# Where the output projection hands over to the up projection: six weight loads in a set order, and two additions of squares moved from GpSimd to VectorE

## The chip, the cores and the metric

The kernel runs on one core of one Trainium2 chip. The metric is the device time of one launch in microseconds (us). The kernel before took 2681.77 us, the median of three runs (2680.84, 2681.77 and 2685.62). Everything is computed in float32 accuracy: each float32 factor is split into a high and a low part of the matmul type fp32r, and three matmuls (high x high, high x low, low x high) make one product.

## The reference, cut to what matters

One layer of a hybrid decoder, for 512 prompt tokens and 8 x 8 sample tokens, 576 columns in all. The mixer's result `mix` goes through the output projection, the sum with the input is normalised, and the feed-forward part begins with the up projection:

```python
def _rmsnorm(x, g):
    y = xf * lax.rsqrt(jnp.mean(xf * xf, axis=-1, keepdims=True) + EPS)
    return (y * g).astype(x.dtype)
...
x = x + jnp.einsum('ble,ed->bld', mix, w_out)        # 2048 -> 2048
h = _rmsnorm(x, norm_ffn_g)
u = jnp.einsum('bld,df->blf', h, w_up)               # 2048 -> 2 x 5632
uc, ffn_new = _causal_dwconv(u, ffn_buf, ffn_conv_w)
gate, up = jnp.split(uc + ffn_conv_b, 2, axis=-1)
x = x + jnp.einsum('blf,fd->bld', jax.nn.silu(gate) * up, w_down)
```

The change touches only the passage from the first of these products to the second: the sums of squares of the new `x` (for the norm) and the first loads of `w_up`.

## The kernel before, in words

Activations lie transposed: 128 features on the partitions, 576 tokens along the free axis, 16 such tiles for 2048 features. The stages follow each other: input projection with the two recurrent heads beside it (to about 1060 us), output projection `w_out` (to about 1150 us), up projection (to about 2140 us), down projection.

**Output projection (`Layer.w_out`).** For each of 16 output tiles a PSUM tile `pd` collects the product (matmuls on line 199). `evac` then loads the input tile from `in_xT` into a buffer `r`, adds the product (VectorE, L1064), writes the sum to DRAM (`x2d`, issued by SyncE a little later through `later`, L188), squares it on ScalarE (`square_acc2`, L1133), adds the square on GpSimd to one of two running sums `acc` (L1134, even and odd tiles), and forms y = x * gain * rstd on VectorE (L1068). Two y tiles together make one group of right operands (`right_operands`): seven combinations of their halves (L1188), each split into `bh` by a ScalarE cast (L119) and `bl` by a VectorE subtraction (L120). There are eight groups. The last two output tiles are computed as a pair (`dense_pair`), so that both their PSUM tiles become complete at the end, and group 7, made of them, is the last.

**Up projection (`ffn`, `pair`, `left_operands`).** A 2 x 2 block of weights times a 2 x 2 block of activations is done in seven products instead of eight. `left_operands` forms seven weight combinations from four loads of 512 KB (a11, a21, a22, a12; L1206), with additions on VectorE (L1230) and the split into `wh` (ScalarE, L119) and `wl` (VectorE, L120). A product is 8 groups x 3 matmuls of 128 x 288 (L1265). For the first pair the first three products (weights a11, a21+a22, and that less a11) are begun on groups 0 to 6, then all three get group 7, then `norm2` puts two matmuls with a matrix of ones on TensorE (L1118), which sum the squares over the partitions; its results scale the outputs later. Then come the other four products.

**What sets the order.** TensorE's order is the order in which the program is written. The other engines' orders come from a scheduler that simulates the program with priorities (`ahead`, `urgent`); `tc.issue_after(ins)` forces what is written inside it behind `ins` on the same engine. Each engine runs its own list strictly in order.

**Buffers.** Loads of `w_up` go to two kinds of buffers: two of the pool `wp`, also used by the loads of `w_out`, and four of `ur`, which lie where the output projection's left activations `ah` and `al` lay, so they can be filled only when the last matmuls no longer read these. Before, every third load goes to `wp`. The tiles `r` of this passage come from a pool of five buffers (`rb`): two hold `acc`, three rotate.

Of the kernel before, what the change touches and what calls it, by code (L numbers as in the profile page):

```python
# [1 line left out]

# [1 line left out]

# [7 lines left out]
ALU = mybir.AluOpType  # L12
# [3 lines left out]
KT = 16  # L16
# [50 lines left out]
class Layer:  # L67
# [967 lines left out]
    def w_out(self, mix):  # L1035


        nc, I = self.nc, self.I
        V = nc.vector
# [14 lines left out]
        both = right(b1, reversed(range(KB1)))[::-1]  # L1054
        self.bh, self.bl = [], []
        self.acc = [self.r(), self.r()]
        ys = []

        def evac(pd):
            n = len(ys)  # L1060
            m = OUT_ORDER[n]
            x = self.r()
            nc.sync.dma_start(out=x, in_=I["xT"][m])
            V.tensor_tensor(out=self.v2(x), in0=self.halves(pd), in1=self.v2(x), op=ALU.add)  # L1064
            self.later(4, self.x2d[m], x)
            self.square_acc2(x, n)
            y = xo.tile([P, NT], F32, tag="y", name=self.nm("y"), bufs=4)
            V.scalar_tensor_tensor(out=y, in0=x, scalar=self.par[:, G2 + m:G2 + m + 1], in1=self.rstd, op0=ALU.mult, op1=ALU.mult)  # L1068
            ys.append(y)

        def operands(k):
            self.right_operands(*both[k], ys[2 * k], ys[2 * k + 1], self.r())

        for k in range(7):
            for i in range(2):
                evac(self.dense())
            if k < KB1:
                operands(k)
            if k == 1:
                pads = lambda t: t[:, 514:594].rearrange("p (b w) -> p b w", b=NB)  # L1080
                nc.gpsimd.memset(self.ratio[:, 0:2], 1.0)
                nc.gpsimd.memset(pads(self.ratio)[:, :, 0:2], 1.0)
                V.reciprocal(self.ratio[:, 2:514], self.rstd[:, 0:SEQ])
                V.reciprocal(pads(self.ratio)[:, :, 2:10], self.rstd[:, SEQ:NT].rearrange("p (b w) -> p b w", b=NB))
# [12 lines left out]
        with self.ahead(OPA):  # L1097
            operands(5)
            operands(6)
            with self.tc.issue_after(self.last_split[0].ins), self.tc.issue_after(self.last_split[1].ins):  # L1100
                evac(pds[0])
                next(steps)
                next(steps)
                evac(pds[1])
                next(steps)
                operands(7)
                V.tensor_tensor(out=self.acc[0], in0=self.acc[0], in1=self.acc[1], op=ALU.add)
        self.finish_jobs()
        self.close("xo")
        return steps  # L1110
# [15 lines left out]
    def square_acc2(self, x, k):  # L1126
        nc = self.nc
        acc = self.acc
        if k < 2:
            nc.scalar.activation(acc[k], x, AF.Square)  # L1130
        else:
            sq = self.r()
            nc.scalar.activation(sq, x, AF.Square)  # L1133
            nc.gpsimd.tensor_tensor(out=acc[k % 2], in0=acc[k % 2], in1=sq, op=ALU.add)  # L1134


    def conv_pads(self, f):
# [62 lines left out]
    def operands(self, early, raws):  # L1200

        def raw(j, t, u):
            pool, n = (self.ur, 4) if self.nraw % 3 else (self.wp, 2)
            self.nraw += 1
            r = raws.pop(0) if raws and n == 4 else pool.tile([P, 1024], F32, tag="raw", name=self.nm("raw"), bufs=n)
            self.nc.sync.dma_start(out=r, in_=self.I["w_up"][2 * j + t][u])  # L1206
            return r

        return self.left_operands(self.ur, 1024, [lambda t, u, j=j: raw(j, t, u) for j in range(NF)], 1, early)
# [434 lines left out]
```

## Time and profile before

| what | value |
|---|---|
| median of the runs | 2681.77 us |
| the profiled execution's own time | 2683.74 us |
| its span from first to last instruction | 2682.0 us |
| TensorE matmul busy | 2638.5 us, 98% |
| VectorE busy | 2079.1 us, 78% |
| ScalarE busy | 1094.6 us, 41% |
| GpSimd busy | 464.5 us, 17% |
| mean granted TensorE clock | 0.997 |

PE is the matmul engine, PEld its weight loads, DVE is VectorE, ACT ScalarE, POOL GpSimd, SPq the DMA queue that SyncE issues. In a timeline row stand the start and the length in microseconds, the engine, the line of the kernel, the operation and its tiles (out<-in, without buffer numbers), and in brackets how long the engine had been idle and what ended that. The lengths of instructions in a row overlap a little (the next one starts before the last has quite ended), so a cost in a chain is best read from one start to the next. TensorE is busy nearly everywhere; what idle time it has around the passage of this change lies between 1150 us and 1171 us.

### The profile page before, as it was taken

To read this page: it belongs to the slowest core of one execution; us is meant where nothing else is said; L and a number is where in the kernel's file an instruction comes from. 1 tells how busy PE (TensorE), PEld (TensorE's weight loads), DVE (VectorE), ACT (ScalarE), POOL (GpSimd) and SP (SyncE) were. 2 spreads that over 40 slices of the span, in tenths; PEclk is the share of its full clock that TensorE was granted. 3 is DMA by queue.
4 is the path that set the end of the run, shared out by engine and by line. 5 is a ranking of instruction groups with operands and counts; after the bars stand their busy time and mean duration, and the time that the engine had idled before them with its cause. 6 is when DMAs were issued, how large, how long until landed. Compare 5 with 4: busy or idle time off the path is not lost.

```text
span 2682.0 us, 48801 instructions
## 1 busy us (share of the span) xinstructions
PE 2638.5 (98%) x19895; PEld 2594.6 (97%) x19895; DVE 2079.1 (78%) x3444; ACT 1094.6 (41%) x1700; POOL 464.5 (17%) x658
## 2 busy tenths in 40 slices
PE   7999999999999999999999999999999999999998
PEld 7998999999999999989999999999999999999997
DVE  7887777765544355489999999999999998988656
ACT  5335344443333232244444444444444443434323
POOL 3222322222211001111111111111111200000001
PEclk9999999999999999999999999999999999999999
DMA  5222222222333433333333333333333373342332
GB/s 196 86 74 94 88 92 92 92 88 90 114 107 99 135 114 131 124 128 113 108 108 108 108 109 108 109 109 111 110 109 109 116 247 95 115 138 72 122 101 97
DMA packets 109865, 299.30 MB, mean 112 GB/s; under 512 B 21624, under 2 KB 27896, under 8 KB 109640
## 3 DMA queue, kind: packets, MB, share of 16 engines
q1 hardware_dynamic: 105592, 286.45, 33.2%
q0 software_dynamic: 1808, 7.37, 0.8%
q8 instruction: 156, 2.56, 0.4%
q10 hardware_dynamic: 2240, 2.36, 0.3%
q14 instruction: 69, 0.57, 0.1%
HBM read 260.07 MB, written 36.06 MB: 110 GB/s over the span
## 4 chain that ended last, share of the span: by engine, by line
PE 88%; DVE 5%; DMA 1%; issue 1%; ACT 0%; POOL 0%; DVEq 0%; SPq 0%; ACTq 0%; POOLq 0%
PE pr L1265 33%; PE pd L199 33%; PE pd L1265 13%; PE pr L199 3%; PE pr L1493 1%; DVE wl L120 1%; DVE bl L120 1%; DMA r<-hid 0%; DVE r L1528 0%; PE pr L843 0%; PE pr L257 0%; PE pr L980 0%; PE pr L982 0%; DVE r L1188 0%; PE pr L855 0%
## 5 line engine op out<-in xcount | busy, mean ns | idle before, releaser
L119 ACT CAST wh<-raw 128x1024 fp32r<-128x1024 f32 (+1 forms) x394 | 405.4, 1029 | 679.3 <-PE pd L199 361.5
L1265 PE MATMUL pr<-bh,wl 128*128 128x288 f32 x2248 | 663.0, 295 | 4.6 <-DVE wl L120 4.6
L1265 PE MATMUL pr<-bh,wh 128*128 128x288 f32 x2248 | 665.2, 296 | 1.2 <-ACT bh L119 1.2
L1265 PE MATMUL pr<-bl,wh 128*128 128x288 f32 x2248 | 662.4, 295 | 0.6 <-DVE bl L120 0.6
L120 DVE TENSOR_TENSOR wl<-raw,wh 128x1024 fp32r<-128x1024 f32 (+1 forms) x394 | 476.5, 1210 | 127.8 <-ACT wh L119 123.7
L199 PE MATMUL pd<-ah,wh 128*128 128x288 f32 x2304 | 518.6, 307 | 0.0
L199 PE MATMUL pd<-ah,wl 128*128 128x288 f32 x2304 | 493.0, 296 | 0.2 <-DVE wl L120 0.2
L199 PE MATMUL pd<-al,wh 128*128 128x288 f32 x2304 | 492.5, 295 | 0.0
L1265 PEld LDWEIGHTS pr<-bh,wl 128*128 128x128 f32 x2248 | 423.5, 188 | 5.8 <-DVE wl L120 5.8
L1265 PEld LDWEIGHTS pr<-bl,wh 128*128 128x128 f32 x2248 | 424.5, 189 | 1.1 <-DVE bl L120 1.1
L1265 PEld LDWEIGHTS pr<-bh,wh 128*128 128x128 f32 x2248 | 422.9, 188 | 1.5 <-ACT bh L119 1.5
L199 PEld LDWEIGHTS pd<-ah,wh 128*128 128x128 f32 x2304 | 369.9, 189 | 14.1 <-issue 7.7
L199 PEld LDWEIGHTS pd<-ah,wl 128*128 128x128 f32 x2304 | 370.5, 189 | 0.5 <-DVE wl L120 0.5
L199 PEld LDWEIGHTS pd<-al,wh 128*128 128x128 f32 x2304 | 370.4, 189 | 0.0
L119 ACT CAST wh<-s 128x1024 fp32r<-128x1024 f32 (+1 forms) x180 | 179.1, 995 | 373.8 <-DVE s L1230 142.5
L1265 PE MATMUL pd<-bh,wh 128*128 128x288 f32 x888 | 262.5, 296 | 0.1
L1265 PE MATMUL pd<-bh,wl 128*128 128x288 f32 x888 | 261.0, 294 | 0.8 <-DVE wl L120 0.8
L1265 PE MATMUL pd<-bl,wh 128*128 128x288 f32 x888 | 260.2, 293 | 0.0
L1148 POOL COPY fst<-r 128x18 f32<-128x18 f32 x88 | 97.6, 1109 | 679.5 <-DVE r L1304 679.5
L120 DVE TENSOR_TENSOR wl<-s,wh 128x1024 fp32r<-128x1024 f32 (+1 forms) x180 | 206.6, 1148 | 6.2 <-ACT wh L119 0.2
L1265 PEld LDWEIGHTS pd<-bh,wl 128*128 128x128 f32 x888 | 166.9, 188 | 1.0 <-DVE wl L120 1.0
L1265 PEld LDWEIGHTS pd<-bl,wh 128*128 128x128 f32 x888 | 167.3, 188 | 0.0
(398 smaller groups left out, 3787.2 us busy)
## 6 DMA issues: line engine op xcount, KB each, us to landing
raw<-in_w_up SPq DMA_DIRECT2D x176, 512.0 KB
raw<-in_w_in SPq DMA_DIRECT2D x114, 512.0 KB
raw<-in_w_down SPq DMA_DIRECT2D x40, 512.0 KB
raw<-in_w_out SPq DMA_DIRECT2D x32, 512.0 KB
raw<-in_w_down SPq DMA_DIRECT2D x40, 384.0 KB
hid<-r SPq DMA_DIRECT2D x44, 288.0 KB
r<-hid SPq DMA_DIRECT2D x40, 288.0 KB
r<-in_xT SPq DMA_DIRECT2D x32, 288.0 KB
```

The source lines that it names most:

```text
L119: self.last_split = (nc.scalar.copy(hi, src), nc.vector.tensor_tensor(out=lo, in0=src, in1=hi.bitcast(F32), op=ALU.subtract))
L120: nc.vector.tensor_tensor(out=lo, in0=src, in1=hi.bitcast(F32), op=ALU.subtract))
L199: mm(outs[hf], w, x[:, hf * HALF:(hf + 1) * HALF], start=first and i == 0, stop=last and i == 2)
L1148: nc.gpsimd.tensor_copy(f, rb[:, 512:602].rearrange("p (b w) -> p b w", b=9)[:, :, 0:2])
L1265: mm(out, w[:, ks], x[:, sl], start=k == 0 and i == 0, stop=k == nk - 1 and i == 2)
L1493: mm(pr[:, 0:n], w[:, ks], acts[kk][:, a * NT + sl.start:a * NT + sl.stop], start=kk == 0 and i == 0, stop=kk == FB - 1 and i == 2)
```

## The change

It does two things.

First, the loads. The rule for the pool of the n-th load of `w_up` changes from every third in `wp` to the first and the last of every six in `wp`; four of six go to `ur` as before. And loads 2 to 7, counted from 1, are each forced behind the one before on SyncE's queue, so that the first loads are issued in the order a11, a21, a22, a12, then a11 and a21 of the next pair, and the next.

Second, the squares. For the last two output tiles `square_acc2` still squares on ScalarE but leaves out the GpSimd addition and returns the square. Where before VectorE added `acc[1]` to `acc[0]`, now it adds the two squares and `acc[1]` to `acc[0]` one after the other, and all three additions are forced behind the last split of group 7.

```diff
@@ Layer.w_out
-        ys = []
+        ys, sq = [], []
@@ evac
-            self.square_acc2(x, n)
+            sq.append(self.square_acc2(x, n))
@@ end of w_out
                 operands(7)
-                V.tensor_tensor(out=self.acc[0], in0=self.acc[0], in1=self.acc[1], op=ALU.add)
+                with self.tc.issue_after(self.last_split[1].ins):
+                    for t in (*sq[-2:], self.acc[1]):
+                        V.tensor_tensor(out=self.acc[0], in0=self.acc[0], in1=t, op=ALU.add)
@@ square_acc2
             sq = self.r()
             nc.scalar.activation(sq, x, AF.Square)
-            nc.gpsimd.tensor_tensor(out=acc[k % 2], in0=acc[k % 2], in1=sq, op=ALU.add)
+            if k < KT - 2:
+                nc.gpsimd.tensor_tensor(out=acc[k % 2], in0=acc[k % 2], in1=sq, op=ALU.add)
+            return sq
@@ raw, in operands
-            pool, n = (self.ur, 4) if self.nraw % 3 else (self.wp, 2)
+            pool, n = (self.ur, 4) if 0 < self.nraw % 6 < 5 else (self.wp, 2)
             self.nraw += 1
             r = raws.pop(0) if raws and n == 4 else pool.tile([P, 1024], F32, tag="raw", name=self.nm("raw"), bufs=n)
-            self.nc.sync.dma_start(out=r, in_=self.I["w_up"][2 * j + t][u])
+            with self.tc.issue_after(self.last_raw.ins) if 1 < self.nraw < 8 else nullcontext():
+                self.last_raw = self.nc.sync.dma_start(out=r, in_=self.I["w_up"][2 * j + t][u])
             return r
```

In the built programs the orders move as follows. (Line numbers of the changed kernel are up to five higher: L1206 becomes L1211, L1188 L1192, L1107 L1109, L1118 L1120, L1265 L1270, L1230 L1235, L1300 L1305.)

SyncE's queue at the handover, before (12598 is a11, 12602 a12, 12557 and 12558 are a21 and a22, 12555 and 12556 the next pair's a11 and a21):

```order
L1206 DMA raw_1570_12598<-in_w_up 128x1024
L1206 DMA raw_1571_12602<-in_w_up 128x1024
L1206 DMA raw_1561_12557<-in_w_up 128x1024
L1206 DMA raw_1562_12558<-in_w_up 128x1024
L1206 DMA raw_1559_12555<-in_w_up 128x1024
L1206 DMA raw_1560_12556<-in_w_up 128x1024
```

And now (12597 is a11, 12557 a21, 12558 a22, 12555 a12, 12556 the next a11, 12727 the next a21):

```order
L1211 DMA raw_1570_12597<-in_w_up 128x1024
L1211 DMA raw_1561_12557<-in_w_up 128x1024
L1211 DMA raw_1562_12558<-in_w_up 128x1024
L1211 DMA raw_1559_12555<-in_w_up 128x1024
L1211 DMA raw_1560_12556<-in_w_up 128x1024
L1211 DMA raw_1584_12727<-in_w_up 128x1024
```

The second load into a buffer of `wp` stood second and now stands last, behind the four into `ur`.

VectorE from the last y product (L1068) on, before (r_1579 is the scratch tile of group 7, r_1399 and r_1400 are the two `acc`, s_1558 the combined weights, wl_1586 the low half of the fourth product's weights):

```order
L1068 SCALAR_TENSOR_TENSOR y_1576_12617<-r_1574_12611,par_82,rstd_90 128x576
L1188 TENSOR_TENSOR r_1579_12624<-y_1569_12596 128x288
L1107 TENSOR_TENSOR r_1399_10616<-r_1399_10616,r_1400_10617 128x576
L1188 TENSOR_TENSOR y_1569_12596<-y_1576_12617,y_1569_12596 128x288
L1188 TENSOR_TENSOR r_1579_12624<-y_1576_12617,r_1579_12624 128x288
L120 TENSOR_TENSOR bl_1564_12563<-y_1576_12617,bh_1563_12562 128x576
L120 TENSOR_TENSOR bl_1564_12563<-y_1569_12596,bh_1563_12562 128x576
L120 TENSOR_TENSOR bl_1564_12563<-r_1579_12624,bh_1563_12562 128x576
L1188 TENSOR_TENSOR y_1576_12617<-y_1576_12617,r_1579_12624 128x288
L1230 TENSOR_TENSOR s_1558_12554<-raw_1571_12602,s_1558_12554 128x1024
L120 TENSOR_TENSOR bl_1564_12563<-y_1576_12617,bh_1563_12562 128x288
L120 TENSOR_TENSOR wl_1586_12730<-raw_1571_12602,wh_1585_12729 128x1024
```

And now, from the same product to the scratch tile's first use, and from there to the third addition to `acc`:

```order
L1068 SCALAR_TENSOR_TENSOR y_1575_12614<-r_1573_12609,par_82,rstd_90 128x576
L1235 TENSOR_TENSOR s_1558_12554<-raw_1559_12555,s_1558_12554 128x1024
L120 TENSOR_TENSOR bl_1564_12563<-y_1575_12614,bh_1563_12562 128x576
L1192 TENSOR_TENSOR r_1578_12621<-y_1569_12595 128x288
L1192 TENSOR_TENSOR y_1569_12595<-y_1575_12614,y_1569_12595 128x288
```

```order
L1192 TENSOR_TENSOR r_1578_12621<-y_1575_12614,r_1578_12621 128x288
L1192 TENSOR_TENSOR y_1575_12614<-y_1575_12614,r_1578_12621 128x288
L120 TENSOR_TENSOR bl_1564_12563<-y_1569_12595,bh_1563_12562 128x576
L120 TENSOR_TENSOR bl_1564_12563<-r_1578_12621,bh_1563_12562 128x576
L120 TENSOR_TENSOR bl_1564_12563<-y_1575_12614,bh_1563_12562 128x288
L1109 TENSOR_TENSOR r_1399_10616<-r_1399_10616,r_1568_12593 128x576
L120 TENSOR_TENSOR wl_1586_12730<-raw_1559_12555,wh_1585_12729 128x1024
L1109 TENSOR_TENSOR r_1399_10616<-r_1399_10616,r_1574_12612 128x576
L120 TENSOR_TENSOR wl_1588_12735<-raw_1561_12557,wh_1587_12734 128x1024
L1109 TENSOR_TENSOR r_1399_10616<-r_1399_10616,r_1400_10617 128x576
```

A weight combination (L1235) and one split of group 7 now stand ahead of the scratch tile's first use, one addition to `acc` has become three, and two weight splits stand between these three.

TensorE's list has the same instructions in the same order; what stands in it as waits differs. Before, where group 7 ends and the two matmuls with ones (L1118) follow:

```order
L1265 MATMUL pr_1584_12654<-bh_1563_12562,wl_1578_12621 128x288
L1118 MATMUL pd_1591_12743<-r_1399_10616,ones_84 128x288 [waits PE_49]
L1118 MATMUL pd_1591_12743<-r_1399_10616,ones_84 128x288
L1265 MATMUL pr_1598_12764<-bh_1397_10614,wh_1585_12729 128x288 [waits Activation_49]
L1265 MATMUL pr_1598_12764<-bl_1398_10615,wh_1585_12729 128x288
L1265 MATMUL pr_1598_12764<-bh_1397_10614,wl_1586_12730 128x288 [waits DVE_49]
```

And now:

```order
L1270 MATMUL pr_1583_12653<-bh_1563_12562,wl_1577_12618 128x288
L1120 MATMUL pd_1591_12743<-r_1399_10616,ones_84 128x288 [waits DVE_49,PE_49]
L1120 MATMUL pd_1591_12743<-r_1399_10616,ones_84 128x288
L1270 MATMUL pr_1598_12764<-bh_1397_10614,wh_1585_12729 128x288 [waits Activation_49]
L1270 MATMUL pr_1598_12764<-bl_1398_10615,wh_1585_12729 128x288
L1270 MATMUL pr_1598_12764<-bh_1397_10614,wl_1586_12730 128x288
```

The wait on VectorE has moved from the fourth product's third matmul to the matmul with ones, three rows earlier. GpSimd's list loses two rows (the two additions), and nothing else of it changes but the order of a DMA and a memset. Behind the third pair of the up projection the orders of VectorE and ScalarE are the same as before; SyncE's differ once more at the very end of that stage, where the first load for the down projection now stands behind four loads of hidden tiles instead of ahead of them.

More of the change, by code (lines that the diff above doesn't have):

```diff
@@ L1 @@
-from contextlib import ExitStack, contextmanager
+from contextlib import ExitStack, contextmanager, nullcontext
 import numpy as np
```

## The prediction

> **What bounds the kernel now.** I read the page's busy times first, then the shares of the chain of waits, and then a table of stages around the handover.
>
> ```profile
> PE 2638.5 (98%) x19895; PEld 2594.6 (97%) x19895; DVE 2079.1 (78%) x3444; ACT 1094.6 (41%) x1700; POOL 464.5 (17%) x658
> PE 88%; DVE 5%; DMA 1%; issue 1%; ACT 0%; POOL 0%; DVEq 0%; SPq 0%; ACTq 0%; POOLq 0%
> ```
>
> TensorE sets the time. An edit elsewhere counts only where TensorE waits for it. In the next table the columns are the stretch, its length, busy time of PE, PEld, DVE, ACT and POOL (with instructions), the granted clock, the DMA share and GB/s.
>
> ```profile
> 1151.00:1155.30 4.30, 1.13 (x9) 0.90 (x8) 3.28 (x4) 1.21 (x2) 0.00 (x0) 1.00 0.64 251
> 1155.30:1158.70 3.40, 3.40 (x16) 3.40 (x15) 3.40 (x3) 0.52 (x1) 1.50 (x1) 0.50 0.53 174
> 1158.70:1164.70 6.00, 5.62 (x42) 5.39 (x41) 6.00 (x7) 2.31 (x3) 1.67 (x2) 1.00 0.49 138
> 1164.70:1171.00 6.30, 3.60 (x19) 2.48 (x18) 6.30 (x11) 4.69 (x8) 0.75 (x2) 1.00 0.00 1
> 1171.00:1180.00 9.00, 9.00 (x69) 9.00 (x70) 9.00 (x15) 4.63 (x6) 0.49 (x2) 1.00 0.65 225
> 1180.00:2060.00 880.00, 880.00 (x6641) 880.00 (x6641) 828.04 (x1111) 399.48 (x438) 171.45 (x238) 1.00 0.34 108
> ```
>
> Up to 1171 TensorE has holes while VectorE is full; from 1171 on TensorE is full for 880 us and more. So there is nothing later in which a gain is lost or a loss made good: what moves TensorE at 1171 moves the end by as much. The holes, with their releasers in brackets:
>
> ```profile
> 1154.44 0.40 PE L1265 MATMUL pr<-bh,wl 128*128 128x288 f32 x1 [3.17 <-DVE wl L120]
> 1162.20 0.40 PE L1265 MATMUL pr<-bh,wl 128*128 128x288 f32 x1 [0.38 <-DVE wl L120]
> 1166.21 0.40 PE L1265 MATMUL pr<-bh,wh 128*128 128x288 f32 x1 [1.24 <-ACT bh L119]
> 1167.21 0.40 PE L1265 MATMUL pr<-bl,wh 128*128 128x288 f32 x1 [0.60 <-DVE bl L120]
> 1168.64 1.13 PE L1118 MATMUL pd<-r,ones 128*128 128x288 f32 x4
> ...
> 1169.75 0.29 PE L1265 MATMUL pr<-bl,wh 128*128 128x288 f32 x1
> 1170.89 0.40 PE L1265 MATMUL pr<-bh,wl 128*128 128x288 f32 x1 [0.85 <-DVE wl L120]
> ```
>
> They sum to 6.24 us, all on VectorE's list or a cast behind it. The matmuls with ones, at 1168.64, carry no bracket: they wait for nothing.
>
> **Part one, the load order: 0 us.** The first hole ends on the split of a11, which VectorE runs behind the sum a21 + a22, and that sum waits for a load:
>
> ```profile
> 1140.30 0.33 SPq L1206 DMA_DIRECT2D raw<-in_w_up  x1
> 1147.03 1.76 SPq L1206 DMA_DIRECT2D raw<-in_w_up  x4
> ...
> 1155.08 0.33 SPq L188 DMA_DIRECT2D x2d<-r  x1
> 1155.50 0.38 SPq L1063 DMA_DIRECT2D r<-in_xT  x1
> 1160.41 0.33 SPq L1206 DMA_DIRECT2D raw<-in_w_up  x1
> 1161.04 0.33 SPq L188 DMA_DIRECT2D x2d<-r  x1
> ```
> ```profile
> 1152.02 1.23 DVE L1230 TENSOR_TENSOR s<-raw,raw 128x1024 f32<-128x1024 f32 x1 [5.54 <-DMA raw<-in_w_up]
> 1153.17 1.22 DVE L120 TENSOR_TENSOR wl<-raw,wh 128x1024 fp32r<-128x1024 f32 x1
> 1154.30 0.75 DVE L1064 TENSOR_TENSOR r<-pd,r 128x576 f32<-128x576 f32 x1
> ```
>
> The order now puts a21 and a22 second and third, but before they were third and fourth behind a load issued 6.7 us earlier, and both versions must wait until 1147.03 for the `ur` buffers. So they land as before and the 3.17 us stay. a12 now comes with them instead of early, needed first at about 1162. Four issues take 1.76 us, 0.44 each, so the sixth load goes out at about 1148.8 and is out of SyncE's way 6 us before the store at 1155.08. Bounds: -0.4 us (one issue pitch less ahead of a22) to +0.4; I take 0, as the wait for the buffers is the same. In the long stage the `wp` and `ur` pattern changes too; no TensorE wait stands in its 880 us, which covers it. Without that cover it is the second rival.
>
> **Part two, the squares: removed.** Two GpSimd additions lie on top of two products on VectorE:
>
> ```profile
> 1155.96 1.50 POOL L1134 TENSOR_TENSOR r<-r,r 128x576 f32<-128x576 f32 x1 [27.19 <-ACT r L1133]
> 1161.86 1.57 POOL L1134 TENSOR_TENSOR r<-r,r 128x576 f32<-128x576 f32 x1 [4.40 <-ACT r L1133]
> 1165.32 0.10 POOL L1142 MEMSET r<- 128x2 f32 x1 [1.74 <-DMA x2d<-r]
> ```
> ```profile
> 1130.12 0.81 DVE L1068 SCALAR_TENSOR_TENSOR y<-r,par,rstd 128x576 f32<-128x576 f32 x1
> ...
> 1156.10 1.98 DVE L1068 SCALAR_TENSOR_TENSOR y<-r,par,rstd 128x576 f32<-128x576 f32 x1
> 1158.00 1.21 DVE L1230 TENSOR_TENSOR s<-s,raw 128x1024 f32<-128x1024 f32 x1
> 1159.13 1.21 DVE L1230 TENSOR_TENSOR raw<-raw,raw 128x1024 f32<-128x1024 f32 x1
> ...
> 1162.07 1.97 DVE L1068 SCALAR_TENSOR_TENSOR y<-r,par,rstd 128x576 f32<-128x576 f32 x1
> 1163.97 0.44 DVE L1188 TENSOR_TENSOR r<-y 128x288 f32<-128x288 f32 x1
> 1164.34 0.74 DVE L1107 TENSOR_TENSOR r<-r,r 128x576 f32<-128x576 f32 x1
> 1165.01 0.44 DVE L1188 TENSOR_TENSOR y<-y,y 128x288 f32<-128x288 f32 x1
> ...
> 1169.62 2.34 DVE L120 TENSOR_TENSOR wl<-raw,wh 128x1024 fp32r<-128x1024 f32 x2
> 1171.90 1.21 DVE L120 TENSOR_TENSOR wl<-s,wh 128x1024 fp32r<-128x1024 f32 x1
> ```
>
> The product takes 0.81 us with GpSimd idle and 1.97 with it adding. I take 0.81: two products, 2 x 1.1 = 2.2 us off VectorE's chain, 1.1 by the first and 1.1 by the second.
>
> **Part two: added.** From start to start (the rows overlap a little) a 1024 wide operation takes 1159.13 - 1158.00 = 1.13 us, a 576 wide one 0.67, a 288 wide one 0.37. By them and the new list: first product 1156.10 to 1156.9, two combinations to 1159.17, addition of the product to the input 1159.84, split 1160.97, second product 1161.77, s + a12 1162.90, `bl` 1163.57. There the scratch tile begins, 0.4 us before the old 1163.97: the 1.1 us of the second product has gone to the sum with a12, which now stands ahead.
>
> A new wait follows. Both squares now live until the last additions, so of the five `r` buffers the scratch tile gets the one of x15, and must wait until this is stored. Before, the store was issued at 1161.04 and a GpSimd memset that waited for it ran at 1165.32, about 4.2 us later. The store is now issued when x15 is ready 0.4 earlier and the load ahead of it likewise some 1.1 earlier, at about 1159.95, and lands at about 1164.2. So the scratch tile starts between 1163.57 (no wait) and 1164.2; I take the wait.
>
> From its start to the end of the third addition: 0.37 and 0.37 until the ScalarE cast (0.67) of y14 lets `bl` go at +1.6; two `bl` 1.34, the half one 0.37, +3.31; then add, split, add, split, add: 3 x 0.67 + 2 x 1.13 = 4.27, and 0.07 until the last has quite ended: +7.65. That is 1171.2 to 1171.85. The matmuls with ones now wait for it, where before they ran at 1168.64. The fourth product's second matmul (1169.75) began 1.11 us after them; its third, whose weights are now split in time, another 0.13 (69 matmuls in 9.00 us): +1.25, so 1172.45 to 1173.1 where it was 1170.89. **That is +1.6 to +2.2; I take +1.9.** The small holes at 1162 to 1168 shift and shrink, but they lie ahead of the new hole and are swallowed by it. Behind the additions on VectorE is the next weight split, at 1171.90 before: the list now reaches it at 1171.8, no later, since the sum with a12 (1.13) has gone ahead and the addition of 0.67 before the first `bl` is gone; so nobody behind waits more. Bounds: if the product stays at 1.97 the chain is 2.2 later, +3.8; if additions and splits hide, nothing is lost (first rival).
>
> **The clock.** The hole of 3.17 us was followed by 3.40 us at a granted clock of 0.50, with 16 matmuls where 3.40 x 69/9.00 = 26 would have run: 10 x 0.13 = 1.3 us lost. The new hole stands in front of the ones. Group 7's last matmul ran until the ones at 1168.64; it now comes about 0.5 us sooner (the scratch tile starts up to 0.2 us later, but the addition of 0.67 behind it is gone), so the hole reaches from about 1168 to 1171.8, 3.8 us. The table's 1158.70:1164.70, with small holes only, kept 1.00. So the loss is 0 (it stays full) to 1.7 (half of 3.40); I take 1.3. [...]
>
> **Sum.** 2683.74 (the profiled execution's own time) + 0 + 1.9 + 1.3 = 2686.9. That execution was 1.97 above the median of the runs, so the forecast for a median is 2681.77 + 3.2 = 2685.0. One part in a thousand: 0.2% of the time, 5.4 us, is about what a measurement of this kernel can tell from no change, so this is "the same", on the slow side.
>
> **Rivals.** *The saving reaches TensorE (faster).* If the matmuls with ones do not hold the fourth product, the four later holes close: 0.38 + 1.24 + 0.60 + 0.85 = 3.07, 2678.7. For it: VectorE is the releaser of nearly all of them. Against: the ones stand ahead of that product in TensorE's list and the last addition behind two splits of 1.13. 0.08.
>
> *The long stage begins to wait (slower).* Two `wp` loads now follow each other across every second pair. Place: the loads of each pair; it decides once a load comes later than VectorE's slack, 880 - 828.04 = 52 us over 40 pairs (44 pairs from about 1172 to 2140 are 22 us each, 880/22 = 40), 1.3 us each.
>
> ```profile
> raw<-in_w_up SPq DMA_DIRECT2D x176, 512.0 KB
> ```
>
> Four loads a pair make 44 pairs; half an issue pitch (0.22 us) in each is 9.7, so 2685.0 + 9.7 = 2694.7. For it: VectorE is 94% busy. Against: the DMA share is 0.34 and nothing waits in 880 us. 0.08.
>
> *The change doesn't do what it says.* The product stays at 1.97 for another cause than GpSimd: third matmul +3.8, with the clock +5.1, 2686.9. Against: 0.81 at 1130.12. 0.06.
>
> **How the numbers follow.** Forecast 0.78, with its own range +0 to +4.5: 2681.8 to 2686.3. The first rival ends below, the third just above, the second far above. 2679.5 to 2688.5 takes in the first part of the first rival's cases, the third, and the runs' own scatter, and leaves out most of the second. Faster by over 0.2% needs less than 2676.4, more than the first rival gives: 0.03. Slower needs more than 2687.1: the second rival's 0.08 and 0.04 of upper ends. Same: 0.85.
>
> **What would show it.** Both L1068 near 0.8 us; VectorE held by the store of x15 for up to 0.6 us at the scratch tile; the matmuls with ones held by L1109 for about 4 us; a granted clock of 0.50 behind that; the 3.17 us unchanged; a full TensorE from then on. I am wrong if the ones start before 1170.5, if the first hole moves by over 0.5 us, or if a wait appears after 1180.

## The result, and the profile after

The changed kernel takes 2687.56 us, the median of 20 runs (2685.59 to 2690.93); the kernel before, in 20 runs beside it, 2683.43 (2680.84 to 2686.0). The ratio is 1.0017, 95% interval 1.001 to 1.0024: 4.1 us slower by the medians, where 3.2 were forecast. The profiled execution has a span of 2685.6 us, 3.6 more than before.

The same table of stages as in the prediction, of the changed kernel (stretch, length, busy time of PE, PEld, DVE, ACT, POOL, granted clock, DMA share, GB/s):

```profile
1151.00:1155.30 4.30, 1.26 (x9) 1.26 (x9) 3.67 (x4) 1.61 (x2) 0.00 (x0) 0.95 0.88 351
1155.30:1158.70 3.40, 3.40 (x17) 3.40 (x16) 3.40 (x4) 1.08 (x2) 0.00 (x0) 0.56 0.55 177
1158.70:1164.70 6.00, 5.23 (x40) 5.00 (x38) 5.30 (x9) 1.45 (x3) 0.00 (x0) 1.00 0.49 139
1164.70:1171.00 6.30, 2.00 (x9) 1.31 (x9) 6.27 (x11) 5.81 (x8) 0.87 (x3) 0.81 0.27 90
1171.00:1180.00 9.00, 8.28 (x46) 7.74 (x47) 8.29 (x12) 2.35 (x4) 0.33 (x2) 0.76 0.40 144
1180.00:2060.00 880.00, 880.00 (x6642) 880.00 (x6642) 825.30 (x1110) 398.70 (x437) 174.38 (x235) 1.00 0.34 108
```

From 1180 on nothing differs: TensorE is full in both, with 6642 matmuls against 6641. The loss lies before. The holes of TensorE, from its timeline:

```profile
1154.04 0.40 PE L1270 MATMUL pr<-bh,wl 128*128 128x288 f32 x1 [3.04 <-DVE wl L120]
1165.49 0.40 PE L1270 MATMUL pr<-bh,wh 128*128 128x288 f32 x1 [1.56 <-ACT bh L119]
1166.32 0.40 PE L1270 MATMUL pr<-bl,wh 128*128 128x288 f32 x1 [0.42 <-DVE bl L120]
1171.72 2.26 PE L1120 MATMUL pd<-r,ones 128*128 128x288 f32 x4 [3.80 <-DVE r L1109]
```

The first hole is as it was (3.17 before). The holes of 0.38 and 0.85 are gone, and in front of the matmuls with ones (L1120), which waited for nothing before, stands a new one of 3.80 us, ended by the third addition. In all 8.82 us against 6.24. On VectorE:

```profile
1155.70 0.81 DVE L1068 SCALAR_TENSOR_TENSOR y<-r,par,rstd 128x576 f32<-128x576 f32 x1
...
1160.50 0.81 DVE L1068 SCALAR_TENSOR_TENSOR y<-r,par,rstd 128x576 f32<-128x576 f32 x1
1161.23 1.22 DVE L1235 TENSOR_TENSOR s<-raw,s 128x1024 f32<-128x1024 f32 x1
...
1163.79 0.46 DVE L1192 TENSOR_TENSOR r<-y 128x288 f32<-128x288 f32 x1 [0.67 <-DMA x2d<-r]
...
1167.22 0.75 DVE L1109 TENSOR_TENSOR r<-r,r 128x576 f32<-128x576 f32 x1
1167.89 1.22 DVE L120 TENSOR_TENSOR wl<-raw,wh 128x1024 fp32r<-128x1024 f32 x1
1169.03 0.75 DVE L1109 TENSOR_TENSOR r<-r,r 128x576 f32<-128x576 f32 x1
1169.69 1.22 DVE L120 TENSOR_TENSOR wl<-raw,wh 128x1024 fp32r<-128x1024 f32 x1
1170.83 0.75 DVE L1109 TENSOR_TENSOR r<-r,r 128x576 f32<-128x576 f32 x1
```

Both L1068 are down from 1.97 to 0.81 us; the scratch tile waits 0.67 us for the store of x15 (`x2d<-r`); two splits lie between the three additions. And the clock, in a table of finer stages:

```profile
1167.90:1171.70 3.80, 0.02 (x1) 0.01 (x1) 3.80 (x6) 3.37 (x4) 0.74 (x2) 0.59 0.62 210
1171.70:1175.30 3.60, 3.58 (x11) 3.03 (x12) 3.60 (x5) 0.50 (x1) 0.33 (x2) 0.50 0.84 293
```

Behind the new hole TensorE runs 3.6 us at half clock. The mean of 0.59 in the hole says that the clock had fallen before the hole was over.

**A measure for the experiments.** Effects of one or two microseconds drown in the time of a launch, which scatters by five. So beside the times stands the *passage*: from the last pair of matmuls of the output projection (L199) to the ScalarE copy of the first product of the 41st pair of the up projection. All work in between is the same, TensorE sets the pace, and the first 1150 us are left out. Before and after:

```profile
1150.57 0.43 PE L199 MATMUL pd<-ah,wl 128*128 128x288 f32 x2
...
2056.08 0.39 ACT L1310 COPY p<-pr 128x288 f32<-128x288 f32 x1
```
```profile
1150.31 0.43 PE L199 MATMUL pd<-ah,wl 128*128 128x288 f32 x2
...
2059.80 0.39 ACT L1315 COPY p<-pr 128x288 f32<-128x288 f32 x1
```

905.51 and 909.49: +3.98 us. Taking the holes away leaves 899.27 and 900.67. So of 3.98 us **2.58 are holes and 1.40 are slower work**, put down here to the clock (0.50 over the 3.6 us behind the new hole). It is one execution of each kernel, and as the runs below show, the clock's part is not the same in every execution.

### The profile page after: what moved, and what is told of

It is laid out like the page before. It is cut to its first block, busy times and chain, and to the rows that moved or that the text cites. A ratio compares the mean times of both kernels' runs of the same rounds, so it can differ in the third digit from the quotient of the medians.

```text
span 2685.6 us, 48777 instructions
## 1 busy us (share of the span) xinstructions
PE 2638.9 (98%) x19895; PEld 2595.1 (97%) x19895; DVE 2078.2 (77%) x3446; ACT 1094.4 (41%) x1700; POOL 463.7 (17%) x656
## 4 chain that ended last, share of the span: by engine, by line
PE 88%; DVE 5%; DMA 1%; issue 1%; ACT 0%; POOL 0%; DVEq 0%; SPq 0%; ACTq 0%; POOLq 0%
PE pr L1270 33%; PE pd L199 33%; PE pd L1270 13%; PE pr L199 3%; PE pr L1498 1%; DVE wl L120 1%; DVE bl L120 0%; DMA r<-hid 0%; DVE r L1533 0%; PE pr L843 0%; PE pr L257 0%; PE pr L980 0%; PE pr L982 0%; DVE r L1192 0%; PE pr L855 0%
## 5 line engine op out<-in xcount | busy, mean ns | idle before, releaser
L1270 PE MATMUL pr<-bh,wh 128*128 128x288 f32 x2248 | 665.8, 296 | 1.6 <-ACT bh L119 1.6
L1270 PE MATMUL pr<-bh,wl 128*128 128x288 f32 x2248 | 663.0, 295 | 3.2 <-DVE wl L120 3.2
L1270 PE MATMUL pr<-bl,wh 128*128 128x288 f32 x2248 | 662.7, 295 | 0.4 <-DVE bl L120 0.4
L199 PE MATMUL pd<-ah,wh 128*128 128x288 f32 x2304 | 518.7, 307 | 0.0
L199 PE MATMUL pd<-ah,wl 128*128 128x288 f32 x2304 | 492.8, 295 | 0.2 <-DVE wl L120 0.2
L199 PE MATMUL pd<-al,wh 128*128 128x288 f32 x2304 | 492.4, 295 | 0.0
L1270 PEld LDWEIGHTS pr<-bh,wl 128*128 128x128 f32 x2248 | 423.8, 189 | 3.9 <-DVE wl L120 3.9
L1270 PEld LDWEIGHTS pr<-bl,wh 128*128 128x128 f32 x2248 | 424.9, 189 | 1.0 <-DVE bl L120 0.9
L1270 PEld LDWEIGHTS pr<-bh,wh 128*128 128x128 f32 x2248 | 423.3, 188 | 1.9 <-ACT bh L119 1.8
L199 PEld LDWEIGHTS pd<-ah,wh 128*128 128x128 f32 x2304 | 369.6, 189 | 14.1 <-issue 7.7
L199 PEld LDWEIGHTS pd<-ah,wl 128*128 128x128 f32 x2304 | 370.4, 188 | 0.4 <-DVE wl L120 0.4
L199 PEld LDWEIGHTS pd<-al,wh 128*128 128x128 f32 x2304 | 370.3, 188 | 0.0
L1270 PE MATMUL pd<-bh,wh 128*128 128x288 f32 x888 | 262.5, 296 | 0.0
L1270 PE MATMUL pd<-bh,wl 128*128 128x288 f32 x888 | 261.0, 294 | 0.8 <-DVE wl L120 0.8
L1270 PE MATMUL pd<-bl,wh 128*128 128x288 f32 x888 | 260.2, 293 | 0.0
L1270 PEld LDWEIGHTS pd<-bh,wl 128*128 128x128 f32 x888 | 166.9, 188 | 1.0 <-DVE wl L120 1.0
L1270 PEld LDWEIGHTS pd<-bl,wh 128*128 128x128 f32 x888 | 167.3, 188 | 0.0
```

The costliest lines, as they stand in the source:

```text
L199: mm(outs[hf], w, x[:, hf * HALF:(hf + 1) * HALF], start=first and i == 0, stop=last and i == 2)
L1270: mm(out, w[:, ks], x[:, sl], start=k == 0 and i == 0, stop=k == nk - 1 and i == 2)
```

## The experiments

All times in us. "Rest" is the passage less TensorE's holes in it (and less the filler in the run that has one). A kernel without any half clock in the passage has a rest of 898.1 (the last but two of the table, granted clock 1.00 in every stage up to 2060), so rest - 898.1 is taken as what half clock costs that execution, an estimate. "Before" in a row is the median of the runs of the kernel before beside it.

| run | median | before | ratio, 95% | passage | holes | rest |
|---|---|---|---|---|---|---|
| before | | | | 905.51 | 6.24 | 899.3 |
| the change | 2687.56 | 2683.43 | 1.0017 (1.001 to 1.0024) | 909.49 | 8.82 | 900.7 |
| loads alone | 2682.87 | 2683.60 | 0.9998 (0.9989 to 1.0007) | 905.32 | 6.04 | 899.3 |
| squares alone | 2688.43 | 2683.60 | 1.0017 (1.0008 to 1.0026) | 910.48 | 8.71 | 901.8 |
| ones later | 2683.77 | 2683.60 | 0.9999 (0.999 to 1.0008) | 906.59 | 6.42 | 900.2 |
| hole filled | 2686.97 | 2683.60 | 1.0014 (1.0006 to 1.0023) | 907.91 | 5.19 + 3.85 | 898.9 |
| scratch in y | 2689.11 | 2683.30 | 1.0021 (1.0012 to 1.0029) | 910.41 | 10.55 | 899.9 |
| additions first | 2685.77 | 2683.30 | 1.0008 (0.9999 to 1.0017) | 908.63 | 8.45 | 900.2 |
| a11 first, ones later | 2683.30 | 2683.30 | 1.0000 (0.9991 to 1.0009) | 903.61 | 3.99 | 899.6 |
| all three mends | 2683.30 | 2683.30 | 1.0000 (0.9991 to 1.0009) | 903.73 | 4.69 | 899.0 |
| a11 first, on before | 2682.43 | 2683.81 | 0.9994 (0.9985 to 1.0002) | 904.37 | 4.66 | 899.7 |
| new order, squares on VectorE | 2680.17 | 2683.81 | 0.9984 (0.9975 to 0.9992) | 901.87 | 3.74 | 898.1 |
| new order, GpSimd, ones early | 2689.22 | 2683.81 | 1.0016 (1.0007 to 1.0025) | 909.79 | 8.93 | 900.9 |
| new order, GpSimd, ones later | 2680.31 | 2682.52 | 0.9987 (0.9978 to 0.9996) | 903.70 | 3.35 | 900.4 |

### Which half of the change costs it

The loads alone: before with the new pool rule and the forced order.

```diff
-            pool, n = (self.ur, 4) if self.nraw % 3 else (self.wp, 2)
+            pool, n = (self.ur, 4) if 0 < self.nraw % 6 < 5 else (self.wp, 2)
...
+            with self.tc.issue_after(self.last_raw.ins) if 1 < self.nraw < 8 else nullcontext():
```

> The kernel before with the load order alone (the pool rule and the forced order of the first loads); the squares stay on GpSimd. Theory: the 4.1 us of the change come from the squares, so this run differs from before by 0, within 0.7 us in the span; L1068 stays near 1.97 us, the hole before a11's low half stays near 3.1 us, no hole of more than 2 us stands in front of the matmuls with ones. Rival: the loads cost part of it (the new pattern of buffers, or the forced order): then at least 1.5 us slower than before, with a wait on a load that before does not have.

The squares alone: the changed kernel with these lines as before.

> The changed kernel with the old load order and the old pool rule: the squares alone. Theory: +3.5 to +4.5 us against before, as the whole change, with a hole of 3.5 to 4.2 us in front of the matmuls with ones, released by the third addition, and some 3 us at half clock behind it. Rival (loads cost part): +2.5 us or less.

Loads: passage -0.19, the first hole 3.06, the ones behind no hole. Squares: passage +4.97, time +0.17% as for the whole change, and in the timeline

```profile
1171.85 2.26 PE L1120 MATMUL pd<-r,ones 128*128 128x288 f32 x4 [3.62 <-DVE r L1109]
```

So the loads do nothing that the passage or the times show, and the squares cost everything. Squares alone cost a microsecond more in the passage than the whole change, but with fewer holes (8.71); the difference is in the rest, where that execution had more half clock (about 13.6 us at 0.50 from 1154 on, against 10.2 in that of the change).

### The place of the ones

The changed kernel, with the matmuls with ones moved behind the fourth product.

```diff
-            self.norm2()
...
         ps = product(2)
+        if j == 0:
+            self.norm2()
```

> The changed kernel, with the two matmuls with ones moved behind the fourth product in TensorE's list. Theory: the three additions then lie under the fourth product's 3 us; the hole of 3.80 us shrinks to the wait for the split of a12 (about 1.1 to 1.3 us), the clock stays at 1.00 behind it, and the run is 3.7 to 4.7 us faster than the changed kernel, 0 to 1 us faster than before. Rival: it is not the place of the ones but VectorE's longer list as such (two more additions, 1.3 us) that delays TensorE: then the hole only moves to the fourth product and at most 2 us come back.

The time is that of before (0.9999), the passage 2.9 us shorter than the changed kernel's. The ones no longer wait:

```profile
1163.65 0.40 PE L1270 MATMUL pr<-bh,wh 128*128 128x288 f32 x1 [1.98 <-ACT bh L119]
1164.48 0.61 PE L1270 MATMUL pr<-bl,wh 128*128 128x288 f32 x1 [0.43 <-DVE bl L120]
1167.48 0.61 PE L1270 MATMUL pr<-bh,wl 128*128 128x288 f32 x1 [0.23 <-DVE wl L120]
1172.14 1.13 PE L1120 MATMUL pd<-r,ones 128*128 128x288 f32 x4
```

Holes fall from 8.82 to 6.42, and the rival (at most 2 us back) falls in the times (3.8 by the medians against the change). What the theory got wrong is the clock: this execution ran 6.8 us at half clock from about 1164.3 on, behind the hole of 1.98 us.

```profile
1164.10:1170.90 6.80, 6.19 (x24) 5.84 (x25) 6.73 (x9) 3.65 (x6) 0.86 (x3) 0.51 0.48 155
```

And against before nothing is won. With the ones out of the way, group 7's first matmul starts 15.05 us after the last pair of the output projection, against 15.64 before: of the 2.2 us that L1068 saves, 0.6 reach TensorE there. The hole in front of it is longer than before (1.98 against 1.24) because TensorE comes to it 1.3 us sooner, mostly since its clock stayed full behind the first hole in this execution (1.00 up to 1164.0, where before has 0.50 over 3.4 us).

### The clock's share

28 matmuls whose result the ones overwrite, in the hole of the changed kernel.

```diff
+        for _ in range(28):
+            self.nc.tensor.matmul(pss[0][0], self.bh[0][:, 0:P], self.bh[0][:, 0:HALF], start=True, stop=True)
         for ps, sl in pss:
             self.nc.tensor.matmul(ps, self.ones, self.acc[0][:, sl], start=True, stop=True)
```

> The changed kernel with 28 idle matmuls (one right operand with itself, written to the ones' own PSUM tile, which the ones then overwrite) in front of the matmuls with ones: they fill about 28 x 0.13 = 3.6 us of the 3.80 us hole and move nothing else. If the clock's share of the loss is 1.3 to 1.7 us as worked out, the clock stays at 1.00 and the run is 1.2 to 1.8 us faster than the changed kernel. Rival: the half clock comes from something else than the idle TensorE (the earlier hole of 3 us, say): then the matmuls behind the ones still run at 0.50 and the time is that of the changed kernel, within 0.5 us.

```profile
1168.15 3.85 PE L1120 MATMUL pd<-bh 128*128 128x288 f32 x28
1172.03 1.24 PE L1122 MATMUL pd<-r,ones 128*128 128x288 f32 x4
```
```profile
1172.00:1175.20 3.20, 3.17 (x20) 2.97 (x21) 3.20 (x5) 0.50 (x1) 0.32 (x2) 1.00 0.91 318
```

The ones take 1.24 us instead of 2.26, the matmuls behind them run at full clock (1.00), and the passage is 1.58 us shorter than the changed kernel's. By the medians it is only 0.6 us, within the scatter of either. So with TensorE busy in the hole no half clock came there (1.00 from 1168.15 to 1180, where the change had 0.50 from 1169.0 to 1175.0), and between these two executions that makes 1.58. The clock of the other executions agrees: the mean granted clock is 0.9961 over the 11 of this run and 0.9953 over the 20 of the changed kernel.

### Additions before the splits, and the buffer wait

In one run the three splits after the additions were forced behind them:

```diff
-            for _ in range(3):
-                next(steps)
+            with self.tc.issue_after(self.last_add.ins):
+                for _ in range(3):
+                    next(steps)
             self.norm2()
```

> The changed kernel, with the next three weight splits (and what makes their weights) forced behind the third addition on VectorE, where the changed kernel has two splits between the additions. The matmuls with ones stay ahead of the fourth product. Theory: the additions end about 2.3 us sooner, the hole in front of the ones is 1.5 to 2.5 us, too short for the half clock of 3.4 us behind it, and the fourth product then waits for its split: 2.5 to 4 us faster than the changed kernel, 0 to 1.5 us slower than before. Rival: the splits that now come late hold the fourth and fifth product by as much as the ones gain: then at most 1 us is won.

```profile
1169.38 2.26 PE L1120 MATMUL pd<-r,ones 128*128 128x288 f32 x4 [2.51 <-DVE r L1109]
1193.07 0.41 PE L1270 MATMUL pr<-bh,wl 128*128 128x288 f32 x1 [1.00 <-DVE wl L120]
```

The hole falls from 3.80 to 2.51, as expected, but only 0.9 us come back in the passage (1.8 by the medians), not 2.5 to 4. Two things took it back: the ones ran at half clock all the same (2.26), and the combinations forced to the rear made a hole of 1.00 us in the second pair. The theory that a hole of this length is too short for the half clock is not settled by it: the granted clock was 1.00 up to 1166.5, 0.71 in the next half microsecond and 0.50 after it, so it fell as the hole began (at 1166.9), behind two holes of 1.07 and 0.42 us. No run shows a length below which a hole leaves the clock full: with the loads alone it fell behind holes of 0.42 and 1.27 us.

In the other, the scratch tile of group 7 lies in a `y` buffer that group 6 has done with:

```diff
-                operands(7)
+                self.right_operands(*both[7], ys[14], ys[15], ys[12])
```

> The changed kernel, with the scratch tile of group 7 in a y buffer that group 6 has done with instead of in x15's buffer, so that it doesn't wait for the store of x15. Theory: VectorE's wait of 0.67 us for the store goes, the third addition and the ones come 0.6 to 1.2 us sooner, the hole in front of the ones stays near 3.8 us; so 0.6 to 1.2 us faster than the changed kernel. Rival: the store only fills time in which the right operands wait for something else (the ScalarE casts): then nothing is won.

```profile
1163.60 1.22 DVE L120 TENSOR_TENSOR wl<-raw,wh 128x1024 fp32r<-128x1024 f32 x1 [0.54 <-ACT wh L119]
...
1169.62 2.26 PE L1120 MATMUL pd<-r,ones 128*128 128x288 f32 x4 [5.41 <-DVE r L1109]
```

A miss: 0.9 us longer in the passage instead of 0.6 to 1.2 shorter. The wait for the store is gone and TensorE begins group 7's last matmul 0.8 us sooner, but the scheduler, which orders by its own simulation, now put one more weight split ahead of the last `bl`, and that split waits 0.54 us for its cast. All three splits then stand before the third addition, and the hole in front of the ones grows to 5.41. The wait of 0.67 us was real; taking it away is worth nothing while the ones wait for the end of VectorE's list.

### The first hole

The split of a11 is put before the sum a21 + a22, and both before the addition that empties the first `pd`; once on the change with the ones later, once on the kernel before.

```diff
-                evac(pds[0])
                 next(steps)
+                with self.tc.issue_after(self.last_split[1].ins):
+                    evac(pds[0])
                 next(steps)
...
-            comb(s, a21, a22, ALU.add)
+            with self.tc.issue_after(self.last_split[1].ins) if early and i == 0 else nullcontext():
+                comb(s, a21, a22, ALU.add)
```

> The changed kernel with the ones behind the fourth product, and with the split of a11 and then the sum a21 + a22 forced to stand ahead of the addition of the first of the last two output tiles: a11's low half no longer waits behind the sum, whose load lands at about 1151.6. Theory: the first hole of 3 us goes to under 0.5 us, and part comes back at the next split (the sum's low half, not ready before 1155): 1.0 to 2.0 us faster than the same kernel without it (ones behind the fourth product), 1 to 2 us faster than before. Rival: every later hole grows by what the first one loses, since VectorE's list from the sum on is the bound: then no gain.

> The kernel before (squares on GpSimd, old loads, ones ahead of the fourth product), with the split of a11 and then the sum a21 + a22 forced ahead of the addition of the first of the last two output tiles. It is the counterpart of that mend on the changed kernel with the ones later, which shortened the passage from the last matmul of the output projection on by 1.9 us against before. Theory: that gain is the mend's alone and needs nothing of the change, so 1 to 2.5 us faster than before in the passage. Rival: it needs the two short products (L1068 at 0.81 instead of 1.97 us): then under 0.5 us.

With the change and the ones later (first two rows), and on the kernel before (the next two):

```profile
1153.14 0.40 PE L1272 MATMUL pr<-bh,wh 128*128 128x288 f32 x1 [0.52 <-ACT wh L119]
1154.94 0.40 PE L1272 MATMUL pr<-bh,wl 128*128 128x288 f32 x1 [1.27 <-DVE wl L120]
```
```profile
1154.05 0.40 PE L1267 MATMUL pr<-bh,wh 128*128 128x288 f32 x1 [0.45 <-ACT wh L119]
1155.85 0.40 PE L1267 MATMUL pr<-bh,wl 128*128 128x288 f32 x1 [1.27 <-DVE wl L120]
```

Of the 3 us 1.7 to 1.8 come back at the next product, as the theory had it. The passage is 1.90 and 1.14 us shorter than before's; against the ones later without the mend it is 2.98 shorter, 2.43 of them holes, where 1 to 2 were forecast. The mend needs nothing of the change, then, though a little more is won with it. The times of both can't be told from before's (intervals across 1).

All three mends together:

> The changed kernel with three mends: the ones behind the fourth product, the split of a11 first, and the scratch tile of group 7 in a free y buffer. Theory: the mends add up, since each takes a wait off the same chain: 3 to 5 us faster than before (about 0.15%), 7 to 9 us faster than the changed kernel, with less than 5 us of holes in the handover where before has 6.24 and the change 8.8. Rival: only one of them counts and the others' waits take its place: then within 1.5 us of before.

A miss again: 1.78 us shorter than before in the passage, no more than without the scratch tile's mend, and no difference in the times, though the holes come to 4.69 us, under 5 as forecast. The ones, now behind the fourth product, wait 1.56 us for the third addition, for the same reason as in the run with the scratch tile alone. Mends on one chain did not add up: each gave the scheduler a new order.

### Another order of the first pair's work

The first hole is there because the second and third of the early products need loads that land at about 1152 (in before their sum started at 1152.02, released by the load). a12's load has landed long before (issued at 1140.30; the DMA engines moved nothing from 1143.7 to 1147.5). So: early products of a11, a12 and a21 + a22, then that of a22, then the ones; the other combinations of weights behind group 7's operands.

```diff
             op(a11)
             yield
+            if first:
+                op(a12)
+                yield
...
-                for out, b, op in zip(begun, (0, 4, 5), self.ops):
+                for out, b, op in zip(begun, (0, 2, 4), self.ops):
...
+            begun = dict(zip((0, 2, 4, 6), begun + [self.psr()[:, 0:HALF]]))
+            self.product(begun[6], 6, steps)
```

> The squares' half of the change (old loads), with another order of the first pair's work: the three products begun early are those of a11, a12 and a21 + a22 (a12's load has landed long before), the product of a22 is the fourth and the matmuls with ones stand behind it, the other combinations of weights are formed behind group 7's operands, and group 7's scratch tile is a free y buffer. The same arithmetic otherwise. Theory: TensorE has two products' work (5.5 us) before it needs the loads that land at 1152, so the holes come to 2 to 4 us instead of 6.2 in before and the half clock is not met; 3 to 6 us faster than before. Rival: the late combinations only move the holes behind group 7: within 1.5 us of before.

> The same other order of the first pair's work on the kernel before: squares of the last two tiles on GpSimd, ones ahead of the fourth product (now a22's), scratch tile from the five r buffers. Theory: VectorE's list up to group 7 is 2.2 us longer (L1068 at 1.97) and lies on the path, so this is 1 to 3 us slower than the same order with the squares on VectorE, but still 1 to 4 us faster than before. Rival: with TensorE covered by two products VectorE's 2.2 us are hidden, and the two are the same within 0.7 us: then the change's saving is worth nothing in any order.

> The other order of the first pair's work once more, with the ones behind the fourth product and the scratch tile in a free y buffer as in the kernel of that order with the squares on VectorE, and with the old loads as there; the two now differ in the squares alone (here the last two tiles' squares are added on GpSimd and one addition is left on VectorE). The earlier kernel of this order with GpSimd also had the ones ahead of the fourth product, and there a hole of 6.26 us opened later, so it told nothing of the squares. Theory: TensorE is covered by two products until about 1158, but group 7's operands are late in both, so the longer L1068 shows: 0.5 to 2 us slower than with the squares on VectorE, 2 to 4 us faster than before. Rival: it is hidden, and the two passages agree within 0.5 us; then the squares' move is worth nothing in this order either.

The version with the squares on VectorE is faster than before: ratio 0.9984, interval 0.9975 to 0.9992, passage 3.64 us shorter. Its holes up to the ones, and the stages:

```profile
1161.42 0.40 PE L1283 MATMUL pr<-bh,wh 128*128 128x288 f32 x1 [0.26 <-ACT bh L119]
1162.31 0.40 PE L1283 MATMUL pr<-bl,wh 128*128 128x288 f32 x1 [0.49 <-DVE bl L120]
1163.85 0.40 PE L1283 MATMUL pr<-bh,wh 128*128 128x288 f32 x1 [0.22 <-ACT wh L119]
1165.11 0.40 PE L1283 MATMUL pr<-bh,wl 128*128 128x288 f32 x1 [0.73 <-DVE wl L120]
1169.08 1.21 PE L1122 MATMUL pd<-r,ones 128*128 128x288 f32 x4 [0.76 <-DVE r L1111]
```
```profile
1154.00:1172.00 18.00, 15.55 (x107) 14.23 (x106) 16.44 (x22) 9.52 (x13) 1.25 (x4) 1.00 0.43 163
1172.00:1180.00 8.00, 7.83 (x60) 7.60 (x59) 8.00 (x14) 2.68 (x4) 0.53 (x2) 1.00 0.62 199
```

The first hole is gone and the granted clock stays at 1.00. Two more follow later (0.17 and, in the second pair, 1.11). The gain is that of the new order as a whole: the place of the ones, the late combinations and the free scratch tile came with it and were not tried one by one.

The first version with GpSimd was not fit for the question: the ones stood early in it, and a hole of 6.26 us opened at 1178.92, ended by a VectorE addition of the pair's outputs (1178.32). VectorE was busy nearly without a gap from 1169.36 up to it, with the norm's instructions and five weight combinations and splits; why the scheduler put these first is not known. The second differs from the VectorE version in the squares alone. Its time is the same (2680.31 and 2680.17), its ratio to before 0.9987 (0.9978 to 0.9996). Its passage is 1.83 us longer, but its holes are 0.39 shorter (3.35 and 3.74), so the difference is all clock: 6.8 us at half clock in that execution. The theory (0.5 to 2 us by the longer L1068) has the size of the passage and not its cause: no hole is longer for it. But the rival, two passages within 0.5 us, doesn't hold either, and the clock's part is not that one execution alone: over 11 executions each, the mean granted clock is 0.9968 here and 0.9976 with the squares on VectorE (0.9964 and 0.9965 in the runs of before beside them). Against before the medians are 2.2 and 3.6 us lower, with intervals that overlap. So whether the place of the squares is worth a microsecond in this order, by the clock, stays open.

## Why the prediction was right

**The load order: 0 forecast, -0.19 measured**, in the run with the loads alone. The reason given, that both versions wait for the same buffers, agrees with the first hole (3.17, 3.06, 3.04). No wait appeared behind 1180, so the second rival fell.

**The product: 2 x 1.1 us off VectorE's chain.** Both L1068 at 0.81: the third rival fell. The saving was spent where the working put it: on the sum with a12 ahead of group 7, on the wait for the store, and on two more additions.

**The scratch tile's wait** was forecast between 0 and 0.6 us; it is 0.67. The store was issued at 1159.48 and the tile begun at 1163.79, 4.3 us, as the 4.2 read off before; but the working let both start about 0.2 us later than they did. Since the tile waits for the store, its own list's lead is lost.

**The hole before the ones: +1.9 taken, about +2.3 measured.** This is the mis-sized term. The passage starts 0.26 us earlier in the changed kernel's trace than in that of before, so 0.26 is added here to its times. By the working the third addition ended at 1171.2 to 1171.85, the ones started with its end, and +1.9 was the middle. The ones started at 1171.98, 0.45 later than the middle. Three reasons show in the rows: the scratch tile was begun at 1164.05, 0.17 later than the middle of 1163.57 to 1164.2; from there to the end of the third addition it took 1171.58 - 1163.79 = 7.79, not 7.65; and the ones started 0.14 after that end. The holes as a whole, the measure of the table above, grew by 2.58.

**The clock: 1.3 taken, 1.40 in the passage, 1.58 in the run with the hole filled.** The size was right, in part by luck, and the picture behind it only in part. The prediction had a long hole set off 3.4 us of half clock behind it, as the one hole of 3.17 us in the trace of before was followed by 3.40 us at 0.50. In the trace of the changed kernel the granted clock is 1.00 up to 1168.5 and 0.50 from 1169.0 to 1175.0: it fell about 0.6 us into the hole and stayed down for 6.8 us, and it cost no more than was taken because nearly half of that, 3.2 us, lay under the hole. That the new hole would bring what the old one did was the author's estimate. No run shows a length of hole that decides it: behind first holes of 3.17 (before) and 3.04 us (the change) the clock fell, behind one of 3.06 us (loads alone) it stayed at 1.00; see the last section.

**The sum**: 3.2 forecast, 3.98 in the passage, 4.1 by the medians. The time itself, 2687.56, is 2.6 us above the forecast of 2685.0 and outside the narrower range of 2681.8 to 2686.3; 1.7 of that is the base, as the median of three executions (2681.77) stood for a kernel whose 20 executions gave 2683.43. The prediction also took 0.2% for about the least that a measurement of this kernel can tell from no change. The 20 executions of each told a ratio of 1.0017 (1.001 to 1.0024) from none: the change is slower, by little.

The first rival (the saving reaches TensorE) fell for the reason given against it; the run with the ones later showed that even past the ones the time is no better than before.

**The work queued behind the additions** was forecast to be no later than before: the next split started at 1171.50 (1171.90 before), and no product waited for it.

## What to carry to other kernels

Work taken from a slow helper is worth what the last waiting instruction gains, not what the helper loses: here the engine that took the additions over was the one TensorE was waiting for, and the matmuls that need the sum stood ahead of work that was ready. Look first at what the idle engine could do meanwhile; the new order, which starts the products whose loads have landed, won 3.6 us where the mends of single waits won two at most. Where a scheduler sets the order, each mend must be read in the new order before it is priced, and where an effect is below the scatter of the times, compare a stretch of fixed work in the traces, holes and rest apart.

## What the runs showed that had not been expected

**Half clock came behind short holes, and not always behind long ones.** Eight of these executions have a first hole of 3.00 to 3.27 us. With it the clock fell to 0.50 in four (before 3.17, the change 3.04, squares alone 3.17, hole filled 3.27) and stayed at 1.00 in the other four (loads alone 3.06, ones later 3.00, scratch in y 3.11, additions first 3.24), so the length of the hole does not decide it. In the run with the loads alone the clock stayed full behind a hole of 3.06 us and fell to half behind holes of 0.42 and 1.27:

```profile
1149.20:1152.90 3.70, 0.66 (x6) 0.43 (x4) 2.40 (x3) 1.04 (x1) 0.00 (x0) 1.00 1.02 403
1152.90:1158.50 5.60, 5.55 (x40) 5.32 (x40) 5.60 (x5) 1.39 (x2) 1.51 (x1) 1.00 0.46 159
1158.50:1161.60 3.10, 1.43 (x9) 1.20 (x9) 3.10 (x4) 1.03 (x2) 1.25 (x1) 1.00 0.52 110
1161.60:1165.00 3.40, 3.40 (x16) 3.17 (x14) 3.40 (x7) 1.69 (x3) 0.52 (x3) 0.51 0.38 146
```

In the new order with GpSimd and the ones later, behind holes of 1.19 and 0.60, it was half for 6.8 us:

```profile
1155.00:1161.60 6.60, 4.76 (x31) 3.88 (x29) 6.53 (x10) 3.46 (x5) 1.53 (x2) 1.00 0.13 47
1161.60:1168.40 6.80, 6.13 (x25) 5.75 (x25) 6.00 (x8) 3.16 (x5) 0.65 (x1) 0.50 0.52 163
```

In the runs read in steps of half a microsecond it came in stretches of about 3.4 us (before, loads alone, hole filled, a11 first with the ones later, and the first one each of the change and of squares alone), 6.8 us (the second one of the change, ones later, additions first, new order with GpSimd and the ones later) or 10.2 us (squares alone, from 1167.7 on), and 3.4 us of it cost, by the rests, 1.1 to 1.2 us (one such stretch in the run with the loads, a rest of 899.3 against 898.1; two in the other, 900.4). What decides when it comes stays open. In these traces the clock's loss, estimated by the rests (898.1 to 901.8), runs from 0 to 3.7 us.

For the changed kernel the clock also goes with the scatter of the times. Of its 20 executions, the seven with a mean granted clock of 0.996 took 2686.2 us in the mean, the twelve with 0.995 took 2688.6, and the one with 0.994 took 2690.7. For the kernel before it explains little: of the 33 executions beside the first experiments, the 18 with 0.997 took 2683.5 in the mean and the 14 with 0.996 took 2683.9.

**In another order the cost of GpSimd's addition fell on another VectorE operation.** In the trace of before the products beside the last two additions took 1.98 and 1.97 us. In the run with a11 first on the kernel before, the second product took 0.82 us, and a 288 wide subtraction beside the addition was long in its place:

```profile
1159.52 0.82 DVE L1068 SCALAR_TENSOR_TENSOR y<-r,par,rstd 128x576 f32<-128x576 f32 x1
...
1161.39 1.68 DVE L1189 TENSOR_TENSOR r<-y 128x288 f32<-128x288 f32 x1
```
```profile
1160.62 2.14 POOL L1135 TENSOR_TENSOR r<-r,r 128x576 f32<-128x576 f32 x1 [3.55 <-ACT r L1134]
```

The subtraction took 1.68 us instead of the 0.44 of before, and the addition 2.14 instead of 1.57. The weight split that VectorE had begun at 1160.26, ahead of the addition, kept its 1.22 us.
